# Modulation of the first two k tiles as one pair, a final normalisation on VectorE alone, and the gate multiplied into the output weights

## The chip, the cores and the metric

The kernel runs on one core of a Trainium2 chip. The metric is the device time of one execution in microseconds. The profile shows one execution; its engines are PE (TensorE, with PEld for its weight loads), DVE (VectorE), ACT (ScalarE), POOL (GpSimd) and SP (the queue that starts most transfers).

## The reference, cut to what matters

```
mod = silu(c) @ w_ada + b_ada                     # c: (1, 2048), w_ada: (2048, 6144)
shift, scale, gate = split(mod, 3)
h = layernorm(x) * (1.0 + scale) + shift          # x: (512, 2048)
proj = h @ w_in                                   # w_in: (2048, 7168)
u, v, z_a, q, k, v_b, z_b = split(proj)
y_a = spatial_gating(gelu(u), gelu(v), z_a)       # 1024 columns
y_b = neighbourhood_attention(q, k, v_b) * silu(z_b)   # 16 heads x 64
y = concat(y_a, y_b) @ w_out                      # w_out: (2048, 2048)
out = layernorm(2 ** 0.25 * x + (1.0 + gate) * y, ln_g, ln_b)
```

All arrays are 32-bit floats. Products of the two projections are made of three passes each (high part by high part, and the two mixed ones).

## The kernel before

**Pieces.** The 2048 rows of `w_in` are 16 k tiles of 128; the 512 tokens are four tiles. `x` is loaded, normalised (statistics on DVE, `normalise` on POOL and DVE) and transposed on PE through `ident` into `xt`. A k tile kk then becomes `h_hi` and `h_lo` by `make_h(kk)`, which needs the 128 shift and scale values of that tile, `modc`.

**Modulation.** `modc` of a k tile is a sum over 16 row blocks j of `w_ada`, each scaled by `c_sb[:, j]`. For the first two k tiles `ada_both(kk, rows)` takes the blocks in `rows` with PE (a product with one column, L381, into `acc_ps[1]`) and the others with DVE (L386, into `acc_ps[0]`); the DVE sum comes last, as `even`, over PE as well (L391), and DVE adds the bias (L392). k tile 0 has `rows` (1, 3) and k tile 1 has (3,). All later k tiles go in pairs, by DVE alone (`ada_vector`, `ada_end`). One tile of `w_ada` holds 4 row blocks of one k tile, or 2 of a pair; there are `ADA` = 7 buffers.

**Order.** Generators set the order. `prepare` yields the steps of the modulation; the string `LASTS` mixes its first steps with the normalising of the last token tile, and `split_halves` then splits the first two chunks of `w_in` into `whi` (ACT) and `wlo` (POOL) by halves, one k tile each. `pump` starts the loads; `ada_before` says ahead of which chunk of `w_in` each tile of `w_ada` is loaded: those of k tile 1 ahead of chunk 2. A chunk is two k tiles by 512 columns, and `raw` has `RAW` = 4 buffers.

**First segment.** `first_segment` starts the chunks VZ0 and V with k tile 0 alone, puts the modulation of k tile 1 between (`advance`), with products by zeros as filling (L542), and goes on with k tile 1. The chunks V, U, ZA and KQ0 follow. In the trace the chunk ZA of this segment is the first that reads `xhi`.

**Output.** The 32 chunks of `w_out` are split by `split_w` (ACT L199, DVE L201) three or more ahead. For each of four column groups cg, `evac_o` takes a product from PSUM: times `gate1` (L913), plus ALPHA times x (L914), statistics (L915). In the last group each token tile is followed by `finish(t)`: the variance's root on POOL (L126), the last D - `SPLIT[t]` columns on ACT and POOL (L924 to L926), the others in two halves on DVE (L929, L931), each stored by SP.

Of the kernel before, what the change touches and what calls it, by code (L numbers as in the profile page):

```python
# [16 lines left out]
P = 128  # L17
D = 2048
T = 512
# [26 lines left out]
LASTS = [1, 1, 0, 0, 0, 0, 1, 1]  # L46
# [5 lines left out]
SPLIT = [1280, 1280, 1280, 1536]  # L52
# [19 lines left out]
def hybrid_kernel(ctx: ExitStack, tc: tile.TileContext, x, c, w_ada, b_ada_cols, b_gate, w_in,  # L72
# [103 lines left out]
    def split_w():  # L176
# [11 lines left out]
        _, k0, pieces, lo = what  # L188
        shape = [P, 1024]
        if len(plan) - 6 < at[1] <= len(plan) - 2:  # L190
# [13 lines left out]
    def split_halves():  # L204

        chunks = []
        for n in range(4):
            if n < 2:
                pump()
                _, k0, pieces, _ = plan[at[1]]  # L210
                at[1] += 1
                raw = loaded.pop(0)[1]
                hi, low = [wst.tile([P, 1024], F32R, name=name, tag=name, bufs=SETS) for name in ("whi", "wlo")]
                chunks.append((raw, hi, low, k0, [w for _, w in pieces]))
            raw, hi, low, k0, widths = chunks[n % 2]
            raw_k, hi_k, low_k = [t.rearrange("p (c k w) -> p k c w", k=2, w=widths[0])[:, n // 2] for t in (raw, hi, low)]
            pin(nc.scalar.copy(out=hi_k, in_=raw_k))
            pin(nc.gpsimd.tensor_tensor(out=low_k, in0=raw_k, in1=hi_k.bitcast(F32), op=ALU.subtract))
            if n >= 2:
                ready.append((hi, low, k0, widths))  # L220
            yield
# [85 lines left out]
    def vz_products(wl, last, evac=None):  # L307

        for i in range(4):
            for kl in range(2):  # L310
                mm_vz(res[i], wl, i, kl, False, last and kl == 1)
            if last:
                evac(i, res[i])
            yield
# [20 lines left out]
    with tc.tile_pool(name="ph1", bufs=1) as ph1:  # L335
        hold[0] = ph1
        ada_groups = [(0, 1), (1, 1)] + [(k, 2) for k in EVEN[1:]]
# [15 lines left out]
        for k0, nk in ada_groups:  # L353
            ada_before += [2 if k0 == 1 else 5 * k0 // 2 - 2 * (k0 > 2)] * (4 * nk)
# [7 lines left out]
        zeros = h_lo[:, NK - 1, :P]  # L362
# [5 lines left out]
        def ada_both(kk, rows):  # L368


            acc = acc_ps[0][:, :2 * P].rearrange("p (s w) -> p s w", s=2)
            even = scratch[0][:, :2 * P].rearrange("p (s w) -> p s w", s=2)
            pc = acc_ps[1][:, T - 2:]
            for j0 in range(0, NK, 4):
                wt = ada_next()
                for j in range(j0, j0 + 4):
                    cj = c_sb[:, j:j + 1]
                    if j % 4 in rows:

                        for s in range(2):  # L380
                            pin(nc.tensor.matmul(pc[:, s:s + 1], lhsT=wt[:, j - j0, s, :], rhs=cj, start=j == rows[0] and s == 0,  # L381
                                                 stop=False, skip_group_check=True))
# [7 lines left out]
            for s in range(2):  # L390
                pin(nc.tensor.matmul(pc[:, s:s + 1], lhsT=even[:, s, :], rhs=one, start=False, stop=s == 1, skip_group_check=True))  # L391
            nc.vector.tensor_tensor(out=modc[:, :, kk:kk + 1], in0=pc.rearrange("p (s k) -> p s k", s=2), in1=bada[:, :, kk:kk + 1], op=ALU.add)  # L392
# [22 lines left out]
        def ada_end(k0, nk):  # L415

            pc = acc_ps[0][:, T - 2:] if nk == 1 else bank()[:, :4]
            pc = pc.rearrange("p (s k) -> p s k", s=2)
# [5 lines left out]
            for kk in range(k0, k0 + nk):  # L424
                make_h(kk, nk == 1)
                yield
# [74 lines left out]
        for what in (0, 1, 0, 1, 0, 0):  # L501
# [28 lines left out]
        def first_segment():  # L530

            wz, wv = next_ws(2)
            for i in range(4):
                mm_vz(res[i], wz, i, 0, True, False)
            two = [bank() for _ in range(2)]
            for i in range(2):
                mm3(two[i], wv, i, 0, False, True, False)

            for steps, n in ((4, 3), (1, 5), (1, 0)):
                advance(steps)  # L540
                for _ in range(n):
                    pin(nc.tensor.matmul(res[0], lhsT=zeros, rhs=h_hi[:, 0, :], start=False, stop=False))  # L542
            for i in range(4):
                mm_vz(res[i], wz, i, 1, False, False)
            yield
            for i in range(2):
                mm3(two[i], wv, i, 1, False, False, True)
                sum_evac(V, i, two[i], 0)
                yield
            for i in range(2, 4):  # L550
                yield from sums(V, [wv], i, 0)
            for q in SEGMENTS[0][1][2:]:
                wls = next_ws(1)
                for i in range(4):
                    yield from sums(q, wls, i, 0)

        def segment(s):
            pairs, order = SEGMENTS[s]
            for q in order:
                if q == VZ0:  # L560
                    for _ in pairs:
                        yield from vz_products(next_w(), False)
# [7 lines left out]
        for s in range(len(SEGMENTS) - 1):  # L570
            for _ in (segment(s) if s else first_segment()):
# [474 lines left out]
```

## Time and profile before

| what | value |
|---|---|
| median of 3 runs | 905.0 us (904.85 to 905.48) |
| time of the profiled execution | 904.64 us |
| its span, first to last instruction | 902.9 us |
| PE busy | 871.9 us (97%) |
| DVE busy | 594.4 us (66%) |
| ACT, POOL busy | 321.6 us, 313.4 us |
| mean granted TensorE clock | 0.992 |

The span is 1.7 us shorter than the time of the same execution, and that time is 0.4 us under the median. Busy times are shares of the whole span; the stages at either end differ from the middle.

### The profile page before, as it was taken

How to read it: one execution, taken by the hardware profiler on the slowest of the kernel's cores; microseconds unless marked ns; L12 is line 12 of the kernel's file. 1: busy time of each engine (PE TensorE's matmuls, PEld its weight loads, DVE VectorE, ACT ScalarE, POOL GpSimd, SP SyncE). 2: the span in 40 equal slices, each digit the busy share in tenths (PEclk: the TensorE clock that was granted, in tenths of full speed). 3: DMA queues.
4: the chain of work that ended last, by engine and by line, in shares of the span. 5: the costliest groups of instructions: out<-in, count | busy, mean ns of one | idle time of the engine just before them, and what ended most of it. 6: DMA issues, size and time to landing. Idle time of an engine off the chain costs nothing.

```text
span 902.9 us, 11810 instructions
## 1 busy us (share of the span) xinstructions
PE 871.9 (97%) x4468; PEld 759.0 (84%) x4468; DVE 594.4 (66%) x860; ACT 321.6 (36%) x399; POOL 313.4 (35%) x225
## 2 busy tenths in 40 slices
PE   4999999999999999999999999999999999999993
PEld 3888888987989988898889988998888888888883
DVE  7768889644486554858768676867766625253667
ACT  3464333224441524524271526342352511222200
POOL 5346456434522535143434435342420000000045
PEclk9999999999999999999999999999999999999997
DMA  9999888734333223345444455343332383223213
GB/s 301 336 355 354 285 285 252 246 92 156 94 94 95 85 96 122 118 129 169 134 152 152 146 170 163 117 142 115 116 117 94 113 339 106 95 94 116 72 62 125
DMA packets 107499, 144.56 MB, mean 160 GB/s; under 512 B 7217, under 2 KB 79025, under 8 KB 106673
## 3 DMA queue, kind: packets, MB, share of 16 engines
q1 hardware_dynamic: 103120, 134.25, 46.1%
q10 hardware_dynamic: 4322, 9.55, 3.0%
q8 instruction: 35, 0.57, 0.3%
q14 instruction: 22, 0.18, 0.1%
HBM read 139.58 MB, written 4.19 MB: 159 GB/s over the span
## 4 chain that ended last, share of the span: by engine, by line
PE 65%; POOL 2%; issue 1%; DVE 1%; ACT 1%; DMA 0%; POOLq 0%; SPq 0%; DVEq 0%; ACTq 0%
PE psm L248 52%; PE psm L261 7%; POOL xr L925 1%; PE psx L736 1%; PE psx L688 1%; PE psx L687 1%; PE psx L615 1%; PE psx L734 1%; POOL xr L926 1%; PE psx L735 1%; POOL rs L126 0%; DMA raw<-in_w_in_dram 0%; ACT xr L924 0%; DVE wlo L201 0%; POOLq L1041 0%
## 5 line engine op out<-in xcount | busy, mean ns | idle before, releaser
L199 ACT CAST whi<-raw 128x1024 fp32r<-128x1024 f32 x131 | 137.1, 1050 | 344.5 <-PE psm L248 212.6
L201 DVE TENSOR_TENSOR wlo<-raw,whi 128x1024 fp32r<-128x1024 f32 x94 | 130.3, 1388 | 161.7 <-ACT whi L199 155.9
L248 PE MATMUL psm<-h_hi,whi 128*128 128x512 f32 x444 | 175.1, 395 | 0.4 <-DVE klo L641 0.4
L248 PE MATMUL psm<-h_hi,wlo 128*128 128x512 f32 x444 | 173.8, 391 | 0.0
L248 PE MATMUL psm<-h_lo,whi 128*128 128x512 f32 x444 | 173.7, 391 | 0.0
L201 POOL TENSOR_TENSOR wlo<-raw,whi 128x1024 fp32r<-128x1024 f32 x37 | 88.7, 2404 | 85.4 <-ACT whi L199 56.4
L248 PE MATMUL psm<-whi,h_hi 128*128 128x512 f32 (+1 forms) x296 | 114.7, 388 | 0.0
L248 PE MATMUL psm<-wlo,h_hi 128*128 128x512 f32 (+1 forms) x296 | 114.0, 385 | 0.0
L248 PE MATMUL psm<-whi,h_lo 128*128 128x512 f32 (+1 forms) x296 | 114.0, 385 | 0.0
L248 PEld LDWEIGHTS psm<-h_hi,wlo 128*128 128x128 f32 x444 | 83.7, 188 | 18.0
L248 PEld LDWEIGHTS psm<-h_hi,whi 128*128 128x128 f32 x444 | 83.6, 189 | 16.2 <-issue 0.8
L248 PEld LDWEIGHTS psm<-h_lo,whi 128*128 128x128 f32 x444 | 83.9, 189 | 15.3 <-issue 0.2
L126 POOL TENSOR_TENSOR rs<-vareps,mhalf 128x1 f32<-128x1 f32 x4 | 4.4, 1098 | 203.2 <-DVE vareps L125 203.2
L261 PE MATMUL psm<-whi,h_hi 128*128 128x256 f32 x248 | 71.1, 287 | 1.7 <-ACT h_hi L434 1.2
L248 PEld LDWEIGHTS psm<-wlo,h_hi 128*128 128x128 f32 x296 | 63.6, 215 | 8.5
L248 PEld LDWEIGHTS psm<-whi,h_hi 128*128 128x128 f32 x296 | 63.4, 214 | 8.5
L261 PE MATMUL psm<-whi,h_lo 128*128 128x256 f32 x248 | 70.3, 285 | 0.2 <-DVE h_lo L440 0.2
L248 PEld LDWEIGHTS psm<-whi,h_lo 128*128 128x128 f32 x296 | 63.4, 214 | 8.3
L261 PE MATMUL psm<-wlo,h_hi 128*128 128x256 f32 x248 | 70.1, 283 | 0.0
L407 DVE SCALAR_TENSOR_TENSOR ada<-wada,c_sb,ada 128x512 f32<-128x512 f32 x91 | 64.0, 749 | 4.8 <-DMA wada<-in_w_ada_dram 4.4
L248 PE MATMUL psx<-h_hi,whi 128*128 128x512 f32 x160 | 63.5, 397 | 1.6 <-DVE y_b L517 0.9
L248 PE MATMUL psx<-h_lo,whi 128*128 128x512 f32 x160 | 62.4, 390 | 0.0
(209 smaller groups left out, 1626.4 us busy)
## 6 DMA issues: line engine op xcount, KB each, us to landing
wada<-in_w_ada_dram SPq DMA_DIRECT2D x128, 256.0 KB, 6.0
raw<-in_w_in_dram SPq DMA_DIRECT2D x128, 256.0 KB, 3.1
raw<-in_w_in_dram SPq DMA_DIRECT2D x48, 512.0 KB, 4.1
rawg<-in_w_ada_dram SPq DMA_DIRECT2D x32, 512.0 KB, 4.2
raw<-in_w_out_dram SPq DMA_DIRECT2D x32, 512.0 KB, 3.6
xt<-in_x_dram SPq DMA_DIRECT2D x8, 512.0 KB, 7.3
xr<-in_x_dram ACTq DMA_DIRECT2D x4, 1024.0 KB, 9.3
tt<-in_rpb_dram ACTq DMA_DIRECT2D x16, 128.0 KB, 2.1
```

Of the source, the lines that this page charges most:

```text
L199: nc.scalar.copy(out=hi, in_=raw)
L201: eng.tensor_tensor(out=low, in0=raw, in1=hi.bitcast(F32), op=ALU.subtract)
L248: nc.tensor.matmul(ps, lhsT=a, rhs=b, start=first and j == 0, stop=last and j == 2)
L261: nc.tensor.matmul(ps[:, t * w:(t + 1) * w], lhsT=a, rhs=b[:, cs], start=first and t == 0 and j == 0, stop=last and t == 1 and j == 2)
L407: nc.vector.scalar_tensor_tensor(out=even if j == NK - 2 else acc, in0=wt[:, j - j0], scalar=cj, in1=acc, op0=ALU.mult, op1=ALU.add)
L615: nc.tensor.matmul(ps[:, tok(n)], lhsT=v[n][:, tok(g)], rhs=wsT[:, g, :], start=True, stop=True)
L687: nc.tensor.matmul(po, lhsT=k2[:, h, keys], rhs=q2[:, h, q], start=True, stop=False)
L688: nc.tensor.matmul(po, lhsT=klo[:, h, keys], rhs=q2[:, h, q], start=False, stop=True)
L734: nc.tensor.matmul(ps[:, q], lhsT=v_hi[:, t, h, :], rhs=hi[:, sl], start=t == 0, stop=False, skip_group_check=True)
L735: nc.tensor.matmul(ps[0:64, q], lhsT=v_lo[:, t, h, :], rhs=hi[:, sl], start=False, stop=False, skip_group_check=True)
L736: nc.tensor.matmul(ps[:, q], lhsT=v_hi[:, t, h, :], rhs=lo[:, sl], start=False, stop=t == 3, skip_group_check=True)
L925: nc.gpsimd.tensor_tensor(out=xr[:, t, cs], in0=xr[:, t, cs], in1=gl[:, cs], op=ALU.mult)
```

## The change

Five edits come together. The first two k tiles are one pair in `ada_groups`: 8 tiles of `w_ada` are loaded in one row ahead of the first chunk of `w_in`. `ada_both` sums the pair: odd row blocks on PE, even ones on DVE, and from the fifth tile on three products by zeros follow each tile (`fill`), and four more the last sum. `first_segment` is gone: segment 0 is built like the others, both k tiles of a chunk at once, and `split_halves` splits only the first chunk. In the output, chunks of the column groups 1 to 3 are multiplied by the gate before they are split, and `evac_o` leaves out its multiplication there. `finish` runs on DVE alone, with stores from SP and ACT in turn.

```
-LASTS = [1, 1, 0, 0, 0, 0, 1, 1]
+LASTS = [1, 1, 0, 0, 0, 0, 1, 1, 1, 1, 1, 1]
+WARM = 4
-SPLIT = [1280, 1280, 1280, 1536]
+PIECES = [768, 512, 512, 256]
...
+        if src is w_out_v and pieces[0][0] >= T:
+            c0, w = pieces[0]
+            half = raw.rearrange("p (k w) -> p k w", k=2)
+            nc.vector.tensor_tensor(out=half, in0=half, in1=gate1[:, c0:c0 + w].rearrange("p (o w) -> p o w", o=1).to_broadcast([P, 2, w]), op=ALU.mult)
...
-        ada_groups = [(0, 1), (1, 1)] + [(k, 2) for k in EVEN[1:]]
+        ada_groups = [(k, 2) for k in EVEN]
...
-            ada_before += [2 if k0 == 1 else 5 * k0 // 2 - 2 * (k0 > 2)] * (4 * nk)
+            ada_before += [5 * k0 // 2 - 2 * (k0 > 2)] * (4 * nk)
...
-        def ada_both(kk, rows):
+        def ada_both(k0, nk, warm):
...
+            def products(rows, rhs, first, last):
+                for s in range(2):
+                    for i in range(nk):
+                        pin(nc.tensor.matmul(pc[:, s, i:i + 1], lhsT=rows[:, s, i * P:(i + 1) * P], rhs=rhs, start=first and s + i == 0,
+                                             stop=last and s + i == nk, skip_group_check=True))
+            def fill(n):
+                ps = bank()
+                for _ in range(n):
+                    pin(nc.tensor.matmul(ps, lhsT=zeros[:, :P], rhs=zeros, start=True, stop=True))
...
+                    if j % 2:
+                        products(wt[:, j - j0], cj, j == 1, False)
...
+                if j0 >= warm * step:
+                    fill(3)
                 pump()
                 yield
...
+            products(even, one, False, True)
+            fill(4)
+            nc.vector.tensor_tensor(out=modc[:, :, k0:k0 + nk], in0=pc, in1=bada[:, :, k0:k0 + nk], op=ALU.add)
...
-            for kk, rows in ((0, (1, 3)), (1, (3,))):
-                yield from ada_both(kk, rows)
+            yield from ada_both(0, 2, WARM)
+            for kk in range(2):
                 make_h(kk, True)
                 yield
...
-        for what in (0, 1, 0, 1, 0, 0):
+        for what in (1, 0, 1, 0, 1):
...
-            for _ in (segment(s) if s else first_segment()):
+            for _ in segment(s):
...
-            tmp = ph3.tile([P, T], F32, name="tmpo", tag="tmpo", bufs=2)[:, :ps.shape[-1]]
-            nc.vector.tensor_tensor(out=tmp, in0=ps, in1=gate1[:, cs], op=ALU.mult)
+            tmp = ps
+            if c0 < T:
+                tmp = ph3.tile([P, T], F32, name="tmpo", tag="tmpo", bufs=2)[:, :ps.shape[-1]]
+                nc.vector.tensor_tensor(out=tmp, in0=ps, in1=gate1[:, cs], op=ALU.mult)
...
-            nc.scalar.activation(out=xr[:, t, cs], in_=xr[:, t, cs], func=AF.Identity, scale=rs[:, t:t + 1], bias=nb)
-            nc.gpsimd.tensor_tensor(out=xr[:, t, cs], in0=xr[:, t, cs], in1=gl[:, cs], op=ALU.mult)
-            nc.gpsimd.tensor_tensor(out=xr[:, t, cs], in0=xr[:, t, cs], in1=bl[:, cs], op=ALU.add)
...
+            for n, w in enumerate(PIECES if t == NT - 1 else [1024, 1024]):
+                cs = slice(o, o + w)
+                nc.vector.scalar_tensor_tensor(out=xr[:, t, cs], in0=xr[:, t, cs], scalar=rs[:, t:t + 1], in1=bl[:, cs],
                                                op0=ALU.mult, op1=ALU.add)
+                (nc.scalar if n % 2 else nc.sync).dma_start(out=out_v[t][:, cs], in_=xr[:, t, cs])
+                o += w
```

PE, from the transposes of the last token tile (L487, `psm`) to the second half of the first chunk, before. `ada1` is the PSUM tile of the one-column products, `wada` a tile of `w_ada`, and the chunks VZ0 and V with k tile 0 stand where the line of dots is:

```order
L487 MATMUL psm_315<-ident_83,xt_114 128x128 x4
L381 MATMUL ada1_116<-c_sb_70,wada_253 128x1 x4
L381 MATMUL ada1_116<-c_sb_70,wada_256 128x1 x4
L391 MATMUL ada1_116<-ones_75,gate1_92 128x1 x2
L261 MATMUL psm_359<-whi_339,h_hi_90 128x256
...
L381 MATMUL ada1_116<-c_sb_70,wada_264 128x1 x2
L381 MATMUL ada1_116<-c_sb_70,wada_267 128x1 x2
L381 MATMUL ada1_116<-c_sb_70,wada_270 128x1 x2
L381 MATMUL ada1_116<-c_sb_70,wada_279 128x1 x2
L542 MATMUL psm_359<-h_hi_90,h_lo_91 128x512 x3
L391 MATMUL ada1_116<-ones_75,gate1_92 128x1 x2
```

The same place of the changed kernel (its L499 is the transpose, L387 the product by zeros, L263 the first product of chunk VZ0):

```order
L499 MATMUL psm_313<-ident_83,xt_114 128x128 x4
L381 MATMUL ada1_116<-c_sb_70,wada_253 128x1 x4
L381 MATMUL ada1_116<-c_sb_70,wada_256 128x1 x4
L381 MATMUL ada1_116<-c_sb_70,wada_259 128x1 x4
L387 MATMUL psx_340<-h_lo_91 128x512 x3
L381 MATMUL ada1_116<-c_sb_70,wada_262 128x1 x4
L387 MATMUL psx_352<-h_lo_91 128x512 x3
L381 MATMUL ada1_116<-c_sb_70,wada_265 128x1 x4
L387 MATMUL psx_364<-h_lo_91 128x512 x3
L381 MATMUL ada1_116<-c_sb_70,wada_273 128x1 x4
L387 MATMUL psx_376<-h_lo_91 128x512 x3
L381 MATMUL ada1_116<-ones_75,gate1_92 128x1 x4
```

The products of the first chunk with k tile 0, which stood between the two sums, now stand behind both, and behind four more products by zeros.

ACT, from the last copy of the transposes (`xt`) to the second k tile, before:

```order
L488 COPY xt_114<-psm_315 128x512
L217 CAST whi_339<-raw_259 128x2x256
L434 ACTIVATE h_hi_90<-xt_114,modc_112 128x512
L217 CAST whi_339<-raw_259 128x2x256
L217 CAST whi_348<-raw_262 128x512 x2
L199 CAST whi_366<-raw_282 128x1024
L434 ACTIVATE h_hi_90<-xt_114,modc_112 128x512
```

The same place of the changed kernel:

```order
L500 COPY xt_114<-psm_313 128x512
L446 ACTIVATE h_hi_90<-xt_114,modc_112 128x512
L221 CAST whi_393<-raw_276 128x2x256 x2
L446 ACTIVATE h_hi_90<-xt_114,modc_112 128x512
L206 CAST whi_411<-raw_279 128x1024
```

The first cast of the first chunk's weights stood ahead of `h_hi` of k tile 0 and now stands behind it.

## Rows read from the trace of the kernel before

**Rows 1.** Busy time of each engine in two stretches (count in brackets), granted clock, DMA.
```profile
core 0: us, PE busy (x) PEld busy (x) DVE busy (x) ACT busy (x) POOL busy (x), PEclk, DMA share, GB/s
...
42.00:888.60 846.60, 844.01 (x4296) 734.08 (x4294) 554.65 (x781) 305.77 (x373) 286.40 (x195) 1.00 0.47 153
888.60:902.90 14.30, 0.00 (x0) 0.00 (x0) 9.30 (x14) 0.81 (x1) 7.29 (x4) 0.64 0.32 124
```

**Rows 2.** Timeline of PE at the front: start, duration, instruction, idle before.
```profile
24.43 1.84 PE L381 MATMUL ada<-c_sb,wada 128*128 128x1 f32 x16
26.13 0.58 PE L391 MATMUL ada<-ones,gate 128*128 128x1 f32 x4
27.88 0.39 PE L261 MATMUL psm<-whi,h_hi 128*128 128x256 f32 x1 [1.16 <-ACT h_hi L434]
...
33.77 1.84 PE L381 MATMUL ada<-c_sb,wada 128*128 128x1 f32 x16
35.47 0.94 PE L542 MATMUL psm<-h_hi,h_lo 128*128 128x512 f32 x3
...
37.85 0.39 PE L261 MATMUL psm<-whi,h_hi 128*128 128x256 f32 x1
...
51.24 0.39 PE L248 MATMUL psx<-h_hi,xhi 128*128 128x512 f32 x1
51.47 0.39 PE L248 MATMUL psx<-h_lo,xhi 128*128 128x512 f32 x1
```

**Rows 3.** Timeline of DVE, ACT and POOL at the front, same columns.
```profile
15.59 2.46 DVE L469 BATCH_NORM_STATS2 st<-xt 128x6 f32<-128x512 f32 x4
...
26.75 0.16 DVE L392 TENSOR_TENSOR modc<-ada,bada 128x2 f32<-128x2 f32 x1 [2.02 <-PE ada L391]
27.01 0.81 ACT L434 ACTIVATE h_hi<-xt,modc 128x512 fp32r<-128x512 f32 x1 [1.12 <-DVE modc L392]
...
27.73 1.65 ACT L217 CAST whi<-raw 128x512 fp32r<-128x512 f32 x3
...
28.93 3.75 POOL L218 TENSOR_TENSOR wlo<-raw,whi 128x512 fp32r<-128x512 f32 x3 [1.70 <-ACT whi L217]
```

**Rows 4.** Three stretches of the front, columns as in rows 1.
```profile
29.07:32.45 3.38, 3.38 (x13) 2.90 (x12) 3.17 (x7) 0.31 (x1) 3.38 (x3) 0.50 1.13 306
32.45:37.85 5.40, 5.40 (x35) 4.81 (x33) 3.15 (x7) 1.86 (x2) 2.39 (x2) 1.00 1.08 354
...
45.00:60.00 15.00, 14.74 (x70) 12.40 (x69) 8.67 (x14) 9.95 (x16) 8.41 (x4) 1.00 1.09 355
```

**Rows 5.** Timeline of the last token tile and its end, all engines.
```profile
885.81 3.26 DVE L931 SCALAR_TENSOR_TENSOR xr<-xr,rs,bl 128x640 f32<-128x640 f32 x2
888.30 0.28 PE L248 MATMUL psm<-whi,h_lo 128*128 128x256 f32 x1
891.83 0.43 DVE L914 SCALAR_TENSOR_TENSOR xr<-xr,tmpo 128x256 f32<-128x256 f32 x1
892.76 0.29 DVE L918 BATCH_NORM_AGGREGATE mv<-st 128x2 f32<-128x30 f32 x1
893.31 1.25 POOL L126 TENSOR_TENSOR rs<-vareps,mhalf 128x1 f32<-128x1 f32 x1 [2.58 <-DVE vareps L125]
894.68 1.01 DVE L929 SCALAR_TENSOR_TENSOR xr<-xr,mv,gl 128x768 f32<-128x768 f32 x1
895.61 2.95 DVE L931 SCALAR_TENSOR_TENSOR xr<-xr,rs,bl 128x768 f32<-128x768 f32 x2
899.70 0.33 SPq L934 DMA_DIRECT2D out_dram<-xr  x1
```

**Rows 6.** Groups of instructions by line and shape, 713 to 860 us: busy, mean ns, idle before.
```profile
L201 DVE TENSOR_TENSOR wlo<-raw,whi 128x1024 fp32r<-128x1024 f32 x26 | 31.8, 1223 | 76.8 <-ACT whi L199 76.8
L199 ACT CAST whi<-raw 128x1024 fp32r<-128x1024 f32 x26 | 27.4, 1055 | 104.3 <-PE psm L248 99.3 <-issue 5.0
...
L913 DVE TENSOR_TENSOR tmpo<-psm,gate 128x512 f32<-128x512 f32 x12 | 7.7, 679 | 0.0
```

More of the change, by code (lines that the diff above doesn't have):

```diff
@@ L187, in split_w @@
             return
-        _, k0, pieces, lo = what
+        src, k0, pieces, lo = what
         shape = [P, 1024]
+        if src is w_out_v and pieces[0][0] >= T:
+            c0, w = pieces[0]
+            half = raw.rearrange("p (k w) -> p k w", k=2)
+            nc.vector.tensor_tensor(out=half, in0=half, in1=gate1[:, c0:c0 + w].rearrange("p (o w) -> p o w", o=1).to_broadcast([P, 2, w]), op=ALU.mult)
         if len(plan) - 6 < at[1] <= len(plan) - 2:
@@ L204, in split_halves @@
     def split_halves():
[L206 to L216, printed above, removed]
+        pump()
+        _, k0, pieces, _ = plan[at[1]]
+        at[1] += 1
+        raw = loaded.pop(0)[1]
+        hi, low = [wst.tile([P, 1024], F32R, name=name, tag=name, bufs=SETS) for name in ("whi", "wlo")]
+        ready.append((hi, low, k0, [w for _, w in pieces]))
+        for n in range(2):
+            raw_k, hi_k, low_k = [t.rearrange("p (c k w) -> p k c w", k=2, w=pieces[0][1])[:, n] for t in (raw, hi, low)]
             pin(nc.scalar.copy(out=hi_k, in_=raw_k))
             pin(nc.gpsimd.tensor_tensor(out=low_k, in0=raw_k, in1=hi_k.bitcast(F32), op=ALU.subtract))
-            if n >= 2:
-                ready.append((hi, low, k0, widths))
             yield
@@ L305, in hybrid_kernel, with vz_products @@
     res = []
-    def vz_products(wl, last, evac=None):
+    def vz_products(wl, last, evac=None, first=False):
         for i in range(4):
             for kl in range(2):
-                mm_vz(res[i], wl, i, kl, False, last and kl == 1)
+                mm_vz(res[i], wl, i, kl, first and kl == 0, last and kl == 1)
             if last:
@@ L361, in hybrid_kernel @@
         modc = ph1.tile([P, 2, NK], F32, name="modc")
-        zeros = h_lo[:, NK - 1, :P]
+        zeros = h_lo[:, NK - 1, :]
         nc.vector.memset(zeros.bitcast(F32), 0.0)
@@ L366, in hybrid_kernel @@
         acc_ps = [ps_a.tile([P, T], F32, name=f"ada{i}") for i in range(2)]
-        def ada_both(kk, rows):
[L371 to L374, printed above, removed]
+        def ada_both(k0, nk, warm):
+            w, step = nk * P, 4 // nk
+            acc, even = [t[:, :2 * w].rearrange("p (s w) -> p s w", s=2) for t in (acc_ps[0], scratch[0])]
+            pc = acc_ps[1][:, T - 2 * nk:].rearrange("p (s k) -> p s k", s=2)
+            def products(rows, rhs, first, last):
[7 more added lines that the diff above has]
+                    pin(nc.tensor.matmul(ps, lhsT=zeros[:, :P], rhs=zeros, start=True, stop=True))
+            for j0 in range(0, NK, step):
                 wt = ada_next()
-                for j in range(j0, j0 + 4):
+                for j in range(j0, j0 + step):
                     cj = c_sb[:, j:j + 1]
[L378 to L382, printed above, removed]
+                    if j % 2:
+                        products(wt[:, j - j0], cj, j == 1, False)
                     elif j == 0:
@@ L415, in ada_end @@
         def ada_end(k0, nk):
-            pc = acc_ps[0][:, T - 2:] if nk == 1 else bank()[:, :4]
-            pc = pc.rearrange("p (s k) -> p s k", s=2)
+            pc = bank()[:, :4].rearrange("p (s k) -> p s k", s=2)
             for s in range(2):
@@ L424, in ada_end @@
             for kk in range(k0, k0 + nk):
-                make_h(kk, nk == 1)
+                make_h(kk)
                 yield
@@ L528, in sums @@
             yield
[L530 to L555, printed above, removed]
         def segment(s):
@@ L561, in segment @@
                     for _ in pairs:
-                        yield from vz_products(next_w(), False)
+                        yield from vz_products(next_w(), False, first=s == 0)
                 else:
```

17 lines of the change are left out of this document (4 added, 13 removed).

## The prediction

> **What bounds the kernel now.** I first read the busy time by stretches. Between 42.0 and 888.6 us PE is busy 844.0 of 846.6 us at the full granted clock (1.00, that is 2.4 GHz) [rows 1]: PE is the bound there, and a change to another engine in that stretch is worth nothing unless it makes PE wait. What can be won lies ahead of 42 us and in the last 14.3 us, where PE does nothing [rows 1]. So I price three places: how early PE comes through its first chunks, whether the output stage keeps PE fed, and what follows the last product.
>
> At the front I read PE's timeline. The product that opens chunk ZA, at 51.24 us, is my mark: the chunks VZ0, V and U are done there in both kernels, and later chunks hold the same products. Their work up to it is 24 products of 256 columns and 60 of 512. Two neighbours of 512 columns start 0.23 us apart [rows 2], so this is 12 x 0.23 + 60 x 0.23 = 16.6 us. Before, some of it is done from 27.88 us on with k tile 0 alone, and the rest starts at 37.85 us, when k tile 1 is there [rows 2]. The mark less the work is 51.24 - 16.6 = 34.6 us: as if PE had started then and never waited. The changed kernel must start by 34.6 us, without a wait, to be no later.
>
> **The front, step by step.** The order on PE up to the transposes of the last token tile is the same, two tiles of one-column products included; those transposes end at 24.43 us, where the next one-column products start [rows 2]. From there the new order on PE is fixed: six tiles of four such products, three products by zeros behind each of the last four, and four products of the DVE sum.
> - Eight one-column products take 24.43 to 26.13 us (16 records, since each is recorded twice) [rows 2]: 0.21 us each. Twenty-four take 5.1 us.
> - Three products by zeros take 0.94 us, the last one's tail of some 0.4 us in it, so they start 0.27 us apart [rows 2]; twelve take 3.1 us, between 2.8 (at 0.23) and 3.3.
> - The last sum starts at 24.43 + 5.1 + 3.1 = 32.6 us. Before, two such products started at 26.13 us and `modc` at 26.75 us [rows 2, 3]: 0.62 us, and two more products 0.43: `modc` at 33.7 us.
> - `h_hi` follows 0.26 us later. ACT's next start is 0.72 us behind that [rows 3], and it is now the first cast of the chunk's weights, which stood ahead of `h_hi` before. A cast is some 0.6 us (three in 1.65 [rows 3]): PE's first real product at 33.7 + 0.26 + 0.72 + 0.65 = 35.3 us.
> - POOL makes `wlo` of k tile 0 and then of k tile 1, 1.25 us each (three in 3.75 [rows 3]), from 35.3 us: ready at 36.6 and 37.8. PE has 0.7 us of other products, waits 0.6 us, has six more products of 0.12, and waits 0.5 us for the second. These two waits are new; behind them stands everything else on PE.
>
> ZA then opens at 35.3 + 1.1 + 16.6 = 53.0 us, 1.8 us later than before.
>
> Could the loads be later than this? DVE takes the statistics of the last token tile from 15.59 us [rows 3], so x has landed by 18 us at the latest. The eight tiles of 0.52 MB need 11.8 us at the 355 GB/s of the stretch that loads such pairs [rows 4]: 27.4 to 30 us for the last, whose products come up on PE at 31 us. Loads are hidden, as are DVE's eight sums of the pair. The earlier end of the loads gains nothing either, since PE is the queue that ends last. If PE's cover were gone they would set the start, which is the third rival.
>
> One cost is bounded, not shown: `h_lo` of both k tiles on DVE now runs beside the two `wlo` on POOL. At the end of the kernel, two operations of 768 columns on DVE beside POOL took 2.95 us, where one alone takes 0.93 from start to start [rows 5]. By that half again, one `wlo` of 1.25 us and one `h_lo` would cost 0.6 us together on this path; at the other end nothing. The Trainium skill bears on this (page "SBUF — State Buffer", section "Who interferes with whom"): a VectorE instruction with two SBUF inputs contends with a GpSimd instruction that reads SBUF. By it I would take the whole 0.6 and a net of 1.8 us instead of 2.0. Since `h_lo` overlaps only part of that time, I take 0.4: the front costs **2.2 us**, 1.5 to 2.6 with these bounds.
>
> **The output stage.** 24 chunks get a multiplication of 1024 columns on DVE, some 1.22 us like the subtraction of that size; 13 evacuations lose 0.68 us each [rows 6]: 29.3 less 8.8, 20.5 us more for DVE in some 135 us of three column groups, a quarter of a chunk's 5.5 us of products. It waits there 76.8 us for ACT, and ACT 99.3 us for PE to give back weight buffers [rows 6]; this idle time is the cover. Queued behind a multiplication stand the subtraction of an earlier chunk, read two chunks later, and the evacuations, which get shorter. I cost it at nothing; if the cover were gone at the heads of the three groups, each would pay one multiplication, 3.7 us in all.
>
> **The tail.** PE's last product ends at 888.58 us [rows 5]. Before, DVE is then still at the third token tile: its two operations from 885.81 us take 3.26 us beside POOL [rows 5]. Now that tile costs DVE four operations of 1024 columns. From 0.93 us for 768 (894.68 to 895.61 [rows 5]) I estimate 1.2 us for 1024, 0.65 for 512 and 0.43 for 256. The third tile is then 0.7 + 0.7 + 0.4 + 4.8 = 6.6 us of DVE, and PE has 36 products of 0.23 us, 8.3 us, left when it starts: DVE is free 1.7 us before the last product ends. Behind the last product: add and statistics 2 x 0.45 us (0.43 each alone), aggregate and one small operation 0.4, two of 1024 columns 2.4, which hide POOL's root of 1.25 us [rows 5], then pieces of 768, 512, 512 and 256: 0.93 + 0.65 + 0.65 + 0.43 = 2.66. The last store is issued at 888.6 + 6.4 = 895.0 us. Before, it was issued at 899.70 us [rows 5] and the span ended 3.2 us later. By that the end would be 898.2. But the four stores, 1.05 MB, leave within 1.7 us, and the bytes need 3.0 us at 355 GB/s [rows 4]; of the 3.2 us before, 0.7 were the bytes of that store and 2.5 were not. From the first issue at 893.3 this makes 898.8. I take 898.7: the tail gains **4.2 us**, 3.7 to 4.7.
>
> **Sum.** 902.9 + 2.2 - 4.2 = 900.9 us of span. The profiled execution's own time is 1.7 us above its span, 904.64, and 0.4 us below the median of 905.0; by the median this is 905.0 - 2.0 = **903.0 us**.
>
> **Rivals.**
> - *The clock falls at the front.* Before, PE had one-column products and a wait from 24.43 to 27.88 us, and in 29.07 to 32.45 us the granted clock was 0.50 (1.2 GHz) [rows 2, 4]; that cost nothing, because k tile 1 was waited for anyway. Now there is no such cover. Against it: from 32.45 to 37.85 us one-column products mixed with products by zeros kept 1.00 [rows 4]. For it: the first 2.6 us behind 24.43 hold one-column products alone again. One such stretch loses at most half of 3.38 us, 1.7, and 0.9 if the one-column products, 60% of that time, keep their pace; I take 1.2: 904.2 us. The Trainium skill (page "TensorE: Matmul & The Clock Gate", section "What's actually happening") says half rate is the default and activity releases it; the fall at 29.07 us agrees, and by that rule it all hangs on what the products by zeros count for, which no row shows by itself.
> - *Slower: the clock stays low into the first chunk.* It decides from 3.8 us of loss on, which is 7.6 us at half rate. Three stretches like the one seen, 10.1 us, would lose 5 us: 908 us. The 32.45 to 37.85 row speaks against it, PE's two new waits for `wlo` for it.
> - *The front does not lose.* If the products by zeros took no time of their own, the small products' weight loads running under them, 3.1 us and more of the front would go: start at 32.2 us, ZA near 50, 899.7 us. Rows 2 speak against: before, the product sums and the zeros follow one another, 33.77, 35.47.
>
> **How the numbers follow.** A run of this kernel can tell about 0.2% (1.8 us) from no change. Forecast 0.48: 903.0, by its bounds (1.5 less 4.7, 2.6 less 3.7) 901.8 to 903.9; six tenths of it lie below 903.2. One clock stretch 0.26: 904.2, nearly all within 0.2%. Front without loss 0.12: 899.7. Slower 0.14. Faster: 0.29 + 0.12 + 0.02 = 0.43; slower 0.14; same 0.43. The range of eight in ten leaves out most of the slower case and the far end of the faster one: 900.8 to 905.6.
>
> **What would show it.** Right: a first real product near 35.3 us, ZA near 53.4, no idle on PE between 60 and 888 us beyond today's, the last store 6.4 us behind the last product, no fall of the granted clock between 27 and 37 us. Wrong in the front: PE waiting for loads between 24 and 33 us, or a clock of 0.50 there. Wrong in the output stage: PE idle ahead of a column group, with the multiplication as releaser. Wrong in the tail: DVE still at the third token tile when PE ends, or the last store more than 7 us behind it.

## The result and the profile after

The changed kernel takes 910.5 us (median of 6 runs, 908.7 to 911.3) against 905.1 us before: 1.0054 times the time, 95% interval 1.0041 to 1.0067. The forecast was 903.0 with a range up to 905.6, so it missed by 7.5 us and had the sign wrong. The profiled execution took 908.68 us, the shortest of the six; its span is 906.9 us against 902.9. All sums below are made on the profiled executions, 4.0 us apart.

First the same kind of stretches as in [rows 1, 4], of the changed kernel (columns as there), cut where the granted clock changes, at the opening of ZA and at PE's last product:

```profile
24.06:29.08 5.02, 5.02 (x40) 4.71 (x39) 2.74 (x4) 0.95 (x2) 0.00 (x0) 0.99 1.09 357
29.08:42.64 13.56, 13.56 (x51) 11.81 (x50) 5.31 (x7) 4.44 (x6) 4.18 (x3) 0.50 1.08 352
42.64:57.21 14.57, 14.57 (x70) 13.22 (x69) 10.29 (x16) 5.46 (x9) 4.58 (x3) 1.00 0.68 219
57.21:896.64 839.43, 835.66 (x4257) 725.66 (x4255) 567.89 (x780) 296.95 (x362) 275.75 (x189) 1.00 0.47 150
896.64:906.90 10.26, 0.00 (x0) 0.00 (x0) 6.33 (x10) 0.00 (x0) 1.51 (x1) 0.63 0.32 119
```

Two things stand out. PE has 13.56 us at 0.50 (1.2 GHz), where [rows 4] had 3.38; and the end without PE has shrunk from 14.3 us [rows 1] to 10.26. PE's timeline after, which answers to [rows 2]:

```profile
24.06 2.74 PE L381 MATMUL ada<-c_sb,wada 128*128 128x1 f32 x24
26.66 0.94 PE L387 MATMUL psx<-h_lo 128*128 128x512 f32 x3
27.44 0.95 PE L381 MATMUL ada<-c_sb,wada 128*128 128x1 f32 x8
28.25 1.04 PE L387 MATMUL psx<-h_lo 128*128 128x512 f32 x3
29.08 1.71 PE L381 MATMUL ada<-c_sb,wada 128*128 128x1 f32 x8
30.65 1.63 PE L387 MATMUL psx<-h_lo 128*128 128x512 f32 x3
...
35.06 1.70 PE L381 MATMUL ada<-ones,gate 128*128 128x1 f32 x8
36.62 2.05 PE L387 MATMUL psx<-h_lo 128*128 128x512 f32 x4
38.48 0.75 PE L263 MATMUL psm<-whi,h_hi 128*128 128x256 f32 x2
...
57.21 0.39 PE L250 MATMUL psx<-h_hi,xhi 128*128 128x512 f32 x1
57.44 0.39 PE L250 MATMUL psx<-h_lo,xhi 128*128 128x512 f32 x1
58.74 0.50 PE L250 MATMUL psx<-h_hi,xlo 128*128 128x512 f32 x1 [0.91 <-POOL xlo L208]
```

The order is the one forecast, and PE never waits up to 57.4 us. But from 29.08 us on every step takes twice its time: three products by zeros 1.63 instead of 0.94 us, four one-column products (8 records, each product being recorded twice) 1.70 instead of 0.95. The first real product comes at 38.48 us (forecast 35.3) and runs at half rate too, until 42.64. ZA opens at 57.21 us instead of 51.24: 5.97 us late, where 2.2 were forecast. Right behind its opening stands a wait that [rows 2] does not have, 0.91 us for `xlo`. ACT and POOL there, in the same columns:

```profile
54.69 0.59 ACT L523 COPY y_a<-psx 128x512 f32<-128x512 f32 x1 [0.77 <-PE psx L250]
55.17 1.05 ACT L206 CAST xhi<-raw 128x1024 fp32r<-128x1024 f32 x1
...
56.30 2.38 POOL L208 TENSOR_TENSOR xlo<-raw,xhi 128x1024 fp32r<-128x1024 f32 x1 [9.99 <-ACT xhi L206]
```

ACT's cast `xhi` waits for nothing of its own; it stands in ACT's order behind two copies of U's sums (into `y_a`; the second is the first line above), and these wait for PE. The end, DVE, which answers to [rows 5]:

```profile
896.68 0.42 DVE L901 SCALAR_TENSOR_TENSOR xr<-xr,psm 128x256 f32<-128x256 f32 x1 [1.06 <-PE psm L250]
897.13 0.43 DVE L902 BATCH_NORM_STATS2 st<-xr 128x6 f32<-128x256 f32 x1
897.60 0.29 DVE L905 BATCH_NORM_AGGREGATE mv<-st 128x2 f32<-128x30 f32 x1
...
897.99 2.47 DVE L909 SCALAR_TENSOR_TENSOR xr<-xr,mv,gl 128x1024 f32<-128x1024 f32 x2
900.38 2.73 DVE L914 SCALAR_TENSOR_TENSOR xr<-xr,rs,bl 128x768 f32<-128x768 f32 x4
```

DVE waits for PE there, not the other way round, and its last piece is done at 903.1 us, 6.5 us behind the last product (forecast 6.4).

So that the runs can be compared place by place, four marks are read from PE's timeline in each trace: the opening of ZA; a product that waits about 0.88 us in every kernel (it starts at 210.30 us before); the first product of the gate's sum (703.20 us before); and the start of the last product (888.30). The table gives the distances in us; e6 is left out, since its order differs. Line numbers shift with the edits. Each row is one execution, and the place of ZA alone scatters: with the front of before it lies between 51.24 and 52.43 us, so a difference of less than about 1 us there says little. The expectations of the runs count the output stage up to the end of the last product and the end from there, so their figures are 0.28 us more and 0.28 us less than the table's.

| kernel | ZA opens | ZA to second mark | gate's sum to last product | last product to end | median |
|---|---|---|---|---|---|
| before | 51.24 | 159.06 | 185.10 | 14.60 | 905.1 |
| after | 57.21 | 160.73 | 185.57 | 10.54 | 910.5 |
| e1 new end alone | 51.58 | 159.01 | 186.14 | 10.51 | 902.0 |
| e2 pair front alone | 59.74 | 160.77 | 185.11 | 14.57 | 913.3 |
| e3 no zeros | 53.83 | 160.75 | 186.02 | 10.51 | 905.0 |
| e4 zeros at six tiles, 3 each | 54.15 | 162.00 | 186.36 | 10.51 | 906.6 |
| e5 zeros at six tiles, 2 each | 56.41 | 161.99 | 186.29 | 10.54 | 909.9 |
| e7 new end, no gate in weights | 52.43 | 159.02 | 185.11 | 10.97 | 902.2 |
| e8 gate by GpSimd | 51.95 | 159.01 | 190.77 | 10.52 | 906.9 |
| e9 e4 and early load | 54.78 | 159.58 | 186.31 | 10.51 | 905.3 |
| e10 zeros at first four tiles | 54.10 | 161.98 | 185.94 | 10.49 | 906.1 |
| e11 gate in last group alone | 52.12 | 159.00 | 185.11 | 10.47 | 901.2 |
| e12 e9 and e11 together | 54.88 | 159.54 | 185.11 | 10.46 | 904.3 |

The stretch from the second mark to the gate's sum is the same in before and after (492.90 and 492.85). For the changed kernel the account is thus +5.97 up to ZA, +1.67 behind it, +0.47 in the output stage, -4.06 at the end: +4.0 with the -0.05 between.

### The profile page after: what moved, and what is told of

Its sections match the earlier page's. It is cut to its first block, busy times and chain, and to the rows that moved or that the text cites. A ratio compares the mean times of both kernels' runs of the same rounds, so it can differ in the third digit from the quotient of the medians.

```text
span 906.9 us, 11826 instructions
## 1 busy us (share of the span) xinstructions
PE 880.4 (97%) x4492; PEld 765.9 (84%) x4492; DVE 610.7 (67%) x856; ACT 317.0 (35%) x394; POOL 298.3 (33%) x216
## 4 chain that ended last, share of the span: by engine, by line
PE 63%; DMA 3%; DVE 3%; issue 0%; ACT 0%; DVEq 0%; SPq 0%; ACTq 0%
PE psm L250 51%; PE psm L263 7%; DMA raw<-in_w_out_dram 2%; DVE wlo L208 1%; PE psx L721 1%; PE psx L673 1%; PE psx L672 1%; PE psx L600 1%; PE psx L719 1%; PE psx L720 1%; DVE raw L196 0%; DMA raw<-in_w_in_dram 0%; ACT whi L206 0%; DVE xr L914 0%; DVE tmpo L900 0%
## 5 line engine op out<-in xcount | busy, mean ns | idle before, releaser
L208 POOL TENSOR_TENSOR wlo<-raw,whi 128x1024 fp32r<-128x1024 f32 x38 | 91.4, 2410 | 78.1 <-ACT whi L206 67.6
L263 PE MATMUL psm<-whi,h_hi 128*128 128x256 f32 x248 | 71.4, 289 | 0.5 <-DVE gate L594 0.5
L263 PE MATMUL psm<-wlo,h_hi 128*128 128x256 f32 x248 | 70.8, 286 | 0.0
L263 PE MATMUL psm<-whi,h_lo 128*128 128x256 f32 x248 | 70.4, 285 | 0.0
```

The lines of the kernel that those rows point to most:

```text
L208: eng.tensor_tensor(out=low, in0=raw, in1=hi.bitcast(F32), op=ALU.subtract)
L263: nc.tensor.matmul(ps[:, t * w:(t + 1) * w], lhsT=a, rhs=b[:, cs], start=first and t == 0 and j == 0, stop=last and t == 1 and j == 2)
```

## The experiments

**Theory.** The clock's fall at 29 us, lasting well into the first chunk, is the main loss; a wrong place of `xhi` on ACT and the gate multiplications in the output stage are two smaller ones. **Rivals.** The pair front is slow by its structure, whatever the clock (zeros on PE's path, loads, weights split late); or the new end gives less than it seems.

**e1 and e2: each half alone.** e1 is the kernel before with the new `evac_o`, `finish` and L192 to L196 of after. e2 is the kernel after with the old ones:

```diff
-PIECES = [768, 512, 512, 256]
+SPLIT = [1280, 1280, 1280, 1536]
-        if src is w_out_v and pieces[0][0] >= T:
-            ...
```

> The kernel before with the new end alone: result finished by VectorE in pieces, gate multiplied into the weights of the last three column groups; front as before. If the loss of the change lies in the front and the end gave 4.1 us (10.26 us behind the last product instead of 14.32), this is 905.0 - 4.1 = 900.9 us, ratio 0.9955. If the 0.5 us by which the two traces drift apart between 711 us and the last product is the price of the gate multiplications, it is 901.4. Rival: the end only looks cheap because the front made everything late; then it is nearer 905.

> The changed kernel with the end of the kernel before: pair front alone. If front and end are independent, the loss is the 7.6 us by which the traces stand apart at 711 us: 905.0 + 7.6 = 912.6 from the profiled run, and up to 914.6 from the medians (910.5 + 4.1); ratio 1.008 to 1.0105. ZA opens near 57.2 us, granted clock 0.50 from about 29 to 42 us. If the output stage lost more than it gained, it would be under 912.

Measured: e1 901.96 us, ratio 0.9967 (0.9955 to 0.9979); e2 913.27 us, 1.0088 (1.0074 to 1.0102). The end gives 4.1 us behind the last product in e1 as in after, and with the front of before it does make the kernel faster; the rival on the end falls. But e1 is 1 us slower than hoped: from the gate's sum to the last product it takes 186.14 us instead of 185.10. e2, without the gate in the weights, takes 185.11. The front alone costs 8.1 us of the medians, about what was expected. (ZA opens later in e2 than in after, by 2.5 us: in that execution the clock was 0.72 already in 20 to 25 us, among the transposes. The two kernels have the same front, so this is a difference between executions.)

**e3: no products by zeros at all.**

```diff
-                if j0 >= warm * step:
-                    fill(3)
...
-            fill(4)
```

> The changed kernel without any product by zeros in the pair front (12 between the tiles and 4 behind the sum); the result is the same. Clock theory: the products by zeros did not keep the clock and at half rate cost 6.5 us of PE's path (four groups of 1.6 us, of which the first at 0.94); without them the sum starts when the last tile has landed and is summed, near 31 us, the first real product near 34, half rate until some 4 us later, ZA at 52 to 53.5 us: 904.5 to 906.5. Rival, the products by zeros are needed to bring the clock back: the clock stays low longer into the chunks, ZA not before 55.5 us, 908.5 or more. Rival, loads set the start: first product not before 36.5 us.

Measured: 904.98 us (903.15 to 908.04), 1.0002 (0.9993 to 1.0012), 5.5 us faster than after. Its stretches and PE's timeline:

```profile
25.00:30.00 5.00, 4.92 (x46) 4.83 (x44) 1.86 (x4) 0.80 (x2) 0.00 (x0) 0.98 1.08 362
30.00:40.10 10.10, 8.43 (x36) 7.84 (x37) 7.61 (x10) 4.44 (x6) 5.75 (x4) 0.50 1.08 351
```

```profile
24.85 6.07 PE L381 MATMUL ada<-c_sb,wada 128*128 128x1 f32 x48
30.78 1.87 PE L381 MATMUL ada<-ones,gate 128*128 128x1 f32 x8
34.32 0.79 PE L263 MATMUL psm<-whi,h_hi 128*128 128x256 f32 x2 [1.67 <-ACT whi L221]
```

The clock falls near 30 us, as in after (29.08), and is back at 40.1 instead of 42.64; the real products start at 34.32 instead of 38.48 us. The zeros in their place of the changed kernel held nothing; they only lengthened PE's path, and at half rate.

**e4, e5, e10: the same zeros in other places.** e4 puts three behind each of the six tiles that follow the transposes (6 more), e5 two behind each of the six (as many as after), e10 three behind the first four (as many as after):

```diff
-WARM = 4
+WARM = 2
```

This is e4; e5 and e10 have it too, and one line more each, the first below in e5, the second in e10:

```diff
-                    fill(3)
+                    fill(2)
```

```diff
-                if j0 >= warm * step:
+                if warm * step <= j0 < (warm + 4) * step:
```

> The changed kernel with three products by zeros behind two more tiles, the two right behind the last transposes (6 products more). Clock theory: the fall at 29 us answers the first 2.6 us behind the transposes, which held one-column products alone; with zeros there the clock stays at 1.00, PE pays 6 x 0.25 = 1.5 us more at full rate, but the sum starts at 24.06 + 5.1 + 18 x 0.26 = 33.9 us, the first real product is near 36.6, ZA near 54.3 us: 907.5 by the median of the changed kernel, granted clock 1.00 from 25 to 60 us. Rival, this mix does not hold the clock wherever it stands: 0.50 as before, six more products at 0.5 us, ZA at 58.5 to 60 us, 911.5 to 913.

> The changed kernel with the same number of products by zeros, 12 between the tiles, but two behind each of the six tiles instead of three behind each of the last four: PE's work at the front is the same, only its place changes. If the clock falls because 2.6 us behind the transposes hold one-column products alone, it stays at 1.00 here: last sum at 24.1 + 5.1 + 3.1 = 32.3 us (33.34 with 18 of them in e4), first real product near 35, ZA near 53, 905.5 by the 906.58 of e4 less 1.0. If what counts is how many columns stand in each stretch, two per tile may be too few: the clock falls once more, 0.50 in 30 to 40 us, ZA near 57, 909 to 911.

> The changed kernel with its 12 products by zeros, three to a tile, behind the first four of the six tiles that follow the transposes instead of the last four; PE's work at the front is that of the changed kernel and of e5. If the clock falls only where a stretch of one-column products stands bare, it stays at 1.00 up to 32 us and may fall in the last three tiles and the sum, behind 33 us, with the first real product near 35: ZA at 53 to 54.5 us, 905 to 906.5. If three to a tile hold the clock only while they last and the fall then reaches well into the chunk, ZA is at 55 us or later: 907.5 to 909.

Measured: e4 906.58 us, 1.0018 (1.0010 to 1.0027); e5 909.86, 1.0055 (1.0041 to 1.0069); e10 906.07, 1.0007 (0.9998 to 1.0016). Stretches of e4, then of e5, then of e10:

```profile
25.00:40.00 15.00, 13.52 (x90) 11.60 (x89) 6.79 (x10) 4.45 (x6) 4.01 (x3) 1.00 1.09 356
40.00:54.00 14.00, 14.00 (x66) 12.68 (x65) 10.48 (x16) 5.31 (x9) 4.63 (x3) 1.00 0.87 286
54.00:70.00 16.00, 15.09 (x69) 12.35 (x68) 9.96 (x14) 10.97 (x17) 11.11 (x5) 0.89 0.88 280
```

```profile
25.00:29.00 4.00, 4.00 (x32) 3.74 (x31) 1.20 (x3) 0.03 (x1) 0.00 (x0) 1.00 1.08 359
29.00:39.50 10.50, 10.50 (x39) 8.94 (x39) 3.20 (x5) 2.67 (x5) 1.26 (x2) 0.51 1.09 355
```

```profile
25.00:33.20 8.20, 8.20 (x61) 7.63 (x61) 2.31 (x5) 0.11 (x1) 0.00 (x0) 1.00 1.08 362
33.20:40.20 7.00, 6.36 (x27) 5.43 (x26) 6.57 (x8) 4.34 (x6) 5.70 (x4) 0.54 1.10 349
```

e4 holds 1.00 through the whole front, and is 3.9 us faster than after although PE has six products more to do: with the same work and more, the clock alone makes that difference. It is not the only cure, as e3 shows: without the zeros, and with the clock low, ZA opens as early (53.83 us against 54.15). Nor is it the whole of the front's loss: with the clock held ZA still opens 2.9 us later than before, 1.6 us of it for the six extra products, so the rival on the front's structure is right for a part, the one that the forecast had priced. e5, with as much work as after, lets the clock fall at 29 us as if the zeros were not there; the first alternative expected for it (that only bare one-column stretches matter) was wrong. e10 keeps the clock through the four tiles with three zeros each, loses it at 33.2 us, behind the two bare ones, and has it back at 40.2; ZA and the time lie where its first alternative put them. What e4 shows beside the clock stands at its sum and the first real products:

```profile
33.34 0.95 PE L381 MATMUL ada<-ones,gate 128*128 128x1 f32 x8
34.15 1.17 PE L387 MATMUL psx<-h_lo 128*128 128x512 f32 x4
35.96 0.50 PE L263 MATMUL psm<-whi,h_hi 128*128 128x256 f32 x2 [0.64 <-ACT whi L221]
...
37.33 0.39 PE L263 MATMUL psm<-wlo,h_hi 128*128 128x256 f32 x1 [0.40 <-POOL wlo L222]
...
38.76 0.50 PE L263 MATMUL psm<-wlo,h_hi 128*128 128x256 f32 x2 [0.45 <-POOL wlo L222]
```

With the clock held, the two waits for `wlo` of the forecast are there (0.40 and 0.45 us; 0.6 and 0.5 forecast), and one of 0.64 us for `whi`. In after, at half rate, PE has none of the three.

**e6 and e9: the cast `xhi`.** e6 fixes its place on ACT ahead of the copies of V's sums. e9 instead lets one more load go ahead of the tiles of the next k pair, in L151. Both start from e4. First e6, then e9:

```diff
-        nc.scalar.copy(out=hi, in_=raw)
+        cast = nc.scalar.copy(out=hi, in_=raw)
+        if at[1] == 4:
+            pin(cast)
...
-                nc.scalar.copy(out=acc, in_=ps)
+                copy = nc.scalar.copy(out=acc, in_=ps)
+                if q == V:
+                    pin(copy)
```

```diff
-            room = (RAWG if gate else RAW - 1) - sum(g == gate for g, _ in loaded)
+            room = (RAWG if gate else RAW - (at[0] != 3)) - sum(g == gate for g, _ in loaded)
```

> The kernel of e4 (three products by zeros behind six tiles, clock held) with the cast xhi placed on ACT ahead of the copies of V's and U's sums, where it waits for its load alone; work the same. Theory: PE's wait of 0.91 us for xlo behind the opening of ZA, and the fall of the clock that followed it in the profiled run of e4 (0.77 and 0.89 in 55 to 65 us), come from xhi standing behind two copies of U's sums. Then the wait goes and 906.58 becomes 905.0 to 905.6. Rival: xhi is late because its load lands late; then the wait moves in front of V's copies, PE waits for banks there, and the time is 906.5 or more.

> The kernel of e4 with one more load ahead of the tiles of the next k pair: the weights of ZA's first chunk are asked for right behind U's, seven tiles earlier on SP's queue. By the order of the programs nothing else changes but that xhi moves on ACT from behind two copies of U's sums to ahead of V's copies. e6 moved xhi too, but changed some 200 places on DVE and PE behind it. Theory: PE's 0.91 us for xlo and the idle DMA queue in 50 to 58 us come from that place on ACT; the wait goes (1.2 us from start to start with the lost pipelining), and so does the fall of the clock that followed it in some runs: 906.58 becomes 904.8 to 905.5. Rival: behind the missing wait PE waits for the same length at the next chunk (modc, h_hi of the next k pair, whose tiles now load 1.4 us later): 906.3 or more.

Measured: e6 914.71 us, 1.0107 (1.0093 to 1.0121); e9 905.25 us, 1.0001 (0.9992 to 1.0009). ACT and PE in e6:

```profile
44.83 1.05 ACT L206 CAST xhi<-raw 128x1024 fp32r<-128x1024 f32 x1 [5.77 <-DMA raw<-in_w_in_dram]
46.42 1.05 ACT L206 CAST whi<-raw 128x1024 fp32r<-128x1024 f32 x1 [0.54 <-DMA raw<-in_w_in_dram]
47.37 1.07 ACT L525 COPY s<-psx 128x512 f32<-128x512 f32 x2
```

```profile
48.00 0.62 PE L252 MATMUL psx<-whi,h_hi 128*128 128x512 f32 x1 [1.91 <-ACT s L525]
...
139.61 0.62 PE L252 MATMUL psx<-whi,h_hi 128*128 128x512 f32 x1 [1.12 <-DVE s L533]
158.93 1.39 PE L435 MATMUL psx<-ones,gate 128*128 128x1 f32 x8 [1.84 <-DVE y_b L533]
```

In e6 the wait for `xlo` is gone, and the load turns out to be there at 44.83 us. SP issues it at 38.27 us in e6 and at 37.66 us in e4, so in e4 `xhi` (52.12 us) stood, by this estimate, some 7 us behind data that had landed. But the next cast, `whi`, moved up with it and waits for its own load ahead of V's copies; PE then waits 1.91 us for these, and the order on DVE changed further back too, with new waits of 1 to 2 us. As an experiment on one suspected wait e6 failed: it changed too much. e9 moves one load and one cast and nothing else, and gives the clean answer: no wait for `xlo`, 1.00 in 54 to 70 us where e4 had 0.89, and 1.3 us less. ACT's cast in e9, then the stretch:

```profile
39.56 1.04 ACT L206 CAST xhi<-raw 128x1024 fp32r<-128x1024 f32 x1
```

```profile
54.00:70.00 16.00, 15.95 (x86) 13.51 (x85) 10.93 (x15) 12.28 (x19) 11.09 (x5) 1.00 0.99 319
```

In the table the stretch behind ZA has three values: 159.0 to 159.6 without the wait (before, e9, e12 and all with the front of before), 160.7 with it (after, e2, e3), 162.0 where the clock fell behind it as well (e4, e5, e10). So the wait costs 1.2 us from start to start, 0.91 of it idle, and the fall behind it 1.25 more. The 0.5 us between before (159.06) and e9 (159.58) are not explained by either.

**e7, e8, e11: the gate in the weights.** All have the front of before and the new end. e7 multiplies in the evacuations only; e8 lets GpSimd multiply the weights; e11 does it for the last column group alone:

```diff
-            if c0 < T:
+            if True:
```

This is e7, which has L192 to L196 of after left out as well; e8 and e11 against e1:

```diff
-            nc.vector.tensor_tensor(out=half, in0=half, in1=gate1[:, c0:c0 + w].rearrange("p (o w) -> p o w", o=1).to_broadcast([P, 2, w]), op=ALU.mult)
+            nc.gpsimd.tensor_tensor(out=half, in0=half, in1=gate1[:, c0:c0 + w].rearrange("p (o w) -> p o w", o=1).to_broadcast([P, 2, w]), op=ALU.mult)
```

```diff
-        if src is w_out_v and pieces[0][0] >= T:
+        if src is w_out_v and pieces[0][0] >= 3 * T:
...
-            if c0 < T:
+            if c0 < 3 * T:
```

> The kernel of e1 (front of before, new end) without the gate in the weights: all evacuations multiply by the gate. Theory: of the 1.0 us that e1 loses in the output stage (gate_sum to the last product 186.42 us against 185.38 before), the gate multiplications ahead of the first column group's evacuation are the cause; here it takes 185.4 us. Behind the last product VectorE has one multiplication more for each of the last pieces, 0.43 us each: 10.23 becomes 10.7 to 11.1 us. Together 901.4 to 901.9 against 901.96 of e1, so the gate in the weights is worth nothing either way. Rival, the gate in the weights is what makes the end short: 902.8 or more. Other rival, the 1.0 us has another cause: the output stage stays at 186.4 and the time is 902.4 to 902.9.

> The kernel of e1 with the 24 gate multiplications on GpSimd, which does nothing from 710 to 860 us, instead of VectorE; the result is the same. Theory as in e7: VectorE's queue at the end of the first column group is then as before, PE does not wait there, the output stage takes 185.4 to 185.6 us, the end behind the last product stays at 10.2 us: 900.9. Rival: VectorE and GpSimd slow each other (two operations of 768 columns took 2.95 us beside GpSimd in the kernel before), weights come late: 902 or more.

> The kernel of e1 with the gate in the weights of the last column group alone (8 multiplications instead of 24); the evacuations of the third group and of the second multiply again. If the 0.57 us wait at 762 us is there because a multiplication and a subtraction stand ahead of evacuations that themselves multiply, it moves to the head of the last group and costs the same: output stage 185.8 to 186.4 us, 901.5 to 902.0. If it came from the number of multiplications, the stage takes 185.4 us and the end 10.2 behind the last product: 900.9.

Measured: e7 902.22 us, 0.9964 (0.9952 to 0.9977); e8 906.89, 1.0022 (1.0014 to 1.0031); e11 901.23, 0.9958 (0.9945 to 0.9970). DVE in e1 at the head of the second column group, and PE's wait:

```profile
754.25 1.22 DVE L194 TENSOR_TENSOR raw<-raw,gate 128x1024 f32<-128x1024 f32 x1 [3.78 <-DMA raw<-in_w_out_dram]
755.39 2.35 DVE L206 TENSOR_TENSOR wlo<-raw,whi 128x1024 fp32r<-128x1024 f32 x2
757.66 1.28 DVE L920 TENSOR_TENSOR tmpo<-psm,gate 128x512 f32<-128x512 f32 x2
...
761.99 0.50 PE L253 MATMUL psm<-whi,h_hi 128*128 128x512 f32 x1 [0.57 <-DVE tmpo L920]
```

One multiplication, which starts when its load lands, and two subtractions stand ahead of the four evacuations; PE waits for the third. In e11 the evacuations start at once, behind one subtraction:

```profile
753.43 1.23 DVE L206 TENSOR_TENSOR wlo<-raw,whi 128x1024 fp32r<-128x1024 f32 x1 [4.22 <-ACT whi L204]
754.57 1.28 DVE L920 TENSOR_TENSOR tmpo<-psm,gate 128x512 f32<-128x512 f32 x2
```

The stage takes 185.11 us in e7 and e11, to the hundredth what e2 takes. So the multiplications at that head cost 1.0 us in e1, and 0.47 in after. For it they shorten the end by 0.46 us (10.97 in e7, 10.51 in e1). My first alternative for e11, that the wait moves to the head of the last group, did not come: there the load was earlier, the first multiplication ran at 836.45 us and the evacuations began at 843.34. Of e8's two alternatives the rival came, with a time above before's:

```profile
L194 POOL TENSOR_TENSOR raw<-raw,gate 128x1024 f32<-128x1024 f32 x24 | 63.4, 2649 | 118.7 <-DMA raw<-in_w_out_dram 109.1 <-DVE wlo L206 9.6
L206 DVE TENSOR_TENSOR wlo<-raw,whi 128x1024 fp32r<-128x1024 f32 x26 | 48.0, 1847 | 61.6 <-ACT whi L204 61.6
```

The multiplication takes 2.65 us on GpSimd instead of 1.22 on DVE, DVE's subtraction beside it 1.85 us on the mean instead of 1.22 [rows 6], and PE waits 3.95 us in one place. The Trainium skill (page "SBUF — State Buffer", section "Who interferes with whom") says that a VectorE instruction with two SBUF inputs contends with a GpSimd instruction that reads SBUF; the longer subtraction agrees.

**e12: the repairs together.** e9 with the edit of e11:

```diff
-        if src is w_out_v and pieces[0][0] >= T:
+        if src is w_out_v and pieces[0][0] >= 3 * T:
...
-            if c0 < T:
+            if c0 < 3 * T:
```

> The kernel of e9 (pair front with three products by zeros behind six tiles, early load for ZA) with the gate in the weights of the last column group alone, as in e11. If the three causes are separate and add up, it is e9 less what e11 gained on e1 in the traces (output stage 186.59 us against 185.39): 905.25 - 1.2 = 904.1, 903.9 to 904.6, still 2.7 to 3.3 us behind e11 (901.23), which is what the pair front costs with the clock held and without the new wait. Rival: the loss in the output stage depends on where the weights' loads stand, not on the first group's evacuations, and comes back: 905 or more.

Measured: 904.28 us, 0.9994 (0.9985 to 1.0003). The stage is at 185.11 us, the time is inside the range expected, and the causes add up. The 3.05 us that are left to e11 are what the pair front costs with the clock held, its six extra products by zeros (1.6 us) in it. The best version of the study is e11: the front of before with the new end, 901.23 us.

## Why the prediction was wrong, step by step

- **The front: the step that failed is "the clock falls at the front".** I forecast no fall (0.48) and took the products by zeros to hold 1.00. The rival that came about is the slower one, "the clock stays low into the first chunk", to which I gave 0.14. Two things were wrong in it. The row I set against it, 1.00 in 32.45 to 37.85 us [rows 4], showed a mix behind real products, during which the clock had come back to 1.00; in the changed kernel the mix came behind bare one-column products, and e3 shows that it then held nothing. And its length was taken too short: I counted three stretches like the one seen, 10.1 us; there were 13.56. Its price of 5 us was still near what the fall cost (4.6, below), since PE's waits of e4 are not there at half rate; what brings the time past that rival's 908 us stands in the next points. I had also wondered whether one-column products keep their pace at half clock; they take 1.70 us instead of 0.95. By e4 the fall cost after 3.06 us at ZA, and 1.6 us more for the six extra products (they start 0.26 us apart in e4): about 4.6 of the 5.97 us, good to about 1 us, as ZA scatters by that much between executions. The forecast's front was 3.8 us short and not 4.6, because the rest of it was some 0.85 us better than forecast:
- **The rest of the front's sum held, and on the safe side.** With the clock held and six products more (1.6 us), the sums of the forecast give the first real product at 36.9 and ZA at 55.0 us; e4 has 35.96 and 54.15. Loads set nothing, as forecast: in after DVE was done with the pair's tiles at 28.4 us and then waited 8.35 us for PE.
- **Behind ZA: a step that is missing.** I moved the casts of the first chunk on ACT but did not follow ACT's order to the fourth chunk. Its load is asked for later, `xhi` is placed behind copies that wait for PE: +1.67 us to the second mark. e9 shows the cause of 1.15 us of it (160.73 less 159.58); the other 0.5 stays open.
- **The output stage: forecast nothing, measured 0.47 us, up to 1.3 in other runs.** The bound was right in kind (the head of a group) and large enough (3.7); the value taken was too low. The idle time that I took for cover is an average; at the head of the second group it is not there.
- **The end: forecast -4.2, measured -4.06.** Each step of it holds, DVE's four operations for the third tile and the pieces of the last included.

Together 3.8 too little for the front, 1.67 behind it, 0.47 in the stage and 0.1 at the end, with -0.05 between: 6.0 us, the distance of the profiled execution's span (906.9) from the forecast one (900.9). The other 1.5 us of the miss is open: four of the six runs lie at 910.5 to 911.3 us. A fall of the clock behind the `xlo` wait, as e4, e5 and e10 show it (1.25 us), would be about that size, but no trace of such a run of the changed kernel was taken, and the mean granted clock does not support it: it is 0.988 in all six runs, the short and the long ones alike, where 2.5 us more at half rate would by themselves lower it by 0.001. The Trainium skill (page "TensorE: Matmul & The Clock Gate", section "What's actually happening") says that the number of products at half rate varies from run to run; the scatter of e3 agrees: its trace has the clock low for 10 us, and its runs go from 903.15 us at a mean granted clock of 0.993 to 908.04 at 0.986; e9, with the clock held in its trace, spreads over 1.0 us.

## What to carry to other kernels

When an edit removes real products from a stretch of small ones, price the clock first: take the whole stretch from the last dense work to the next at half rate, small products too, and do not trust filler until a run shows the clock held; filler that fails is worse than none (e3 against after, 5.5 us by the medians). Where a load is asked for later, follow its cast through the engine's order to the chunk that uses it, since a cast behind copies that wait for PE delays PE in turn. And judge cover at the busiest place (the head of a group), not by a mean.

## What was not expected of the hardware

The same twelve products by zeros let the clock fall or held it by where they stood: two behind each of six tiles, it fell at 29 us (e5); three behind each of four, it stood at 1.00 up to 33.2 us, 3 us past the last of them (e10). A wait of 0.91 us on PE was followed by a clock of 0.89 over 54 to 70 us in e4, while the changed kernel, with the same wait, shows 1.00 behind it.
